# Sixteen of 22 gated blocks of a hybrid decoder layer transposed by DMA in uint16 halves

## The chip, the cores and the metric

The kernel runs on one core of one Trainium2 chip. The metric is the device time of one execution in microseconds (us), here the median of three runs. The matmul engine is called TensorE or PE, its weight load PEld, VectorE DVE, ScalarE ACT, GpSimd POOL; SP issues most DMAs, and SPq is its queue of instructions.

## The reference

One decoder layer on 256 tokens of width 2048, all in float32: a SwiGLU feed-forward, a mixer (windowed attention beside RWKV-7), cross-attention into a memory, a second SwiGLU feed-forward, a final norm. The change lies in the two feed-forwards:

```python
def swiglu(h, w_gate, w_up, w_down):
    return (jax.nn.silu(h @ w_gate) * (h @ w_up)) @ w_down
...
    x = x + 0.5 * swiglu(rms_norm(x, ffn1_norm[l]), ffn1_w_gate[l], ffn1_w_up[l], ffn1_w_down[l])
```

`w_gate` and `w_up` are 2048 x 5632 and `w_down` is 5632 x 2048.

## The kernel before

**Numbers in two parts.** Every float32 operand `v` of a matmul is split into `hi` (ACT's copy with type float32r, L370 for weights) and `lo = v - hi` (DVE, L371), and every product is three matmuls: hi by hi, lo by hi, hi by lo (L447 to L449).

**Blocks.** A feed-forward goes through its 5632 hidden columns in 11 blocks of 512, in three groups (4, 4 and 3). `gate_and_up` (L580) makes one block `hb`: 256 tokens by 512 columns, that is two tiles of 128 tokens (t = 0, 1). The tokens lie on the partitions. `down` (L608) multiplies a whole group by `w_down` and needs the hidden columns on the partitions, so each block is transposed in between, and then split into `hhi` and `hlo` by `split` (L642). The first block of a feed-forward comes from two plain products (L762 to L774).

**Eight steps of a block.** `product_pair` (L507) walks K = 2048 in eight steps, q = 0 to 7, of two 128-row slices of both weights. In the steps q of `SEVEN` it computes seven products in place of eight, from sums of weights that DVE makes (`raw`, L399 to L402), which are split as `thi` and `tlo` (L378, L379). In the first feed-forward these are q = 0, 2, 4; in the second q = 0, 2, 3, 4, where the sums of q = 3 were made earlier and are loaded from memory. Right after q = 4, `first` and `middle` (L585 to L593) take the seven-product banks off PSUM, and `out` (L595) closes the block after q = 7.

**Order of the work.** The program is recorded in one pass. Generators in groups (`Interleave`, L56) are stepped by `tick`, which the product calls some 29 times in a block; `idle(n)` lets n ticks pass. The tile framework then sets each engine's order from that record, and each engine executes in its order: an instruction that waits holds up all behind it on that engine. ACT and DVE prepare the parts of a weight one to two steps ahead of PE, in buffers (three for `hi` and `lo`, one for each of the `thi` and `tlo`) that PE has to release. SP loads 1 MB pieces of the weights into four buffers (`raw2`, tag of L311) as DVE releases them: one piece of the gate and one of the up weight feed two steps q.

**The transposes.** `transposed` (L750) calls `feat` (L632) twice, each with four PE transposes of 128 x 128 against `ident` into one PSUM bank, and `split` takes the banks. A block's generator is spawned in `middle` of the following block (L592), so its eight transposes stand on PE behind step q = 4 of that block. The last block of a group is transposed when `down` begins (L777). `sums_of` (L577) hands out `u` tiles, tag "u", two buffers; `hb` has two buffers.

Of the kernel before, what the change touches and what calls it, by code (L numbers as in the profile page):

```python
# [6 lines left out]

F32 = mybir.dt.float32
F32R = mybir.dt.float32r
AF = mybir.ActivationFunctionType  # L10
ALU = mybir.AluOpType
AX = mybir.AxisListType
# [3 lines left out]
P = 128  # L16
# [120 lines left out]
def decoder_layer(ctx: ExitStack, tc: tile.TileContext, a: dict, out: bass.AP):  # L137
    nc = tc.nc
    act, dve, pool, pe = nc.scalar, nc.vector, nc.gpsimd, nc.tensor
# [7 lines left out]
    bg = Interleave()  # L147
# [5 lines left out]
    bg.group("norm", 1)  # L153
    bg.group("mem", 1)
    bg.group("stage", 4)

    def f32(x):
        return x.bitcast(F32)
# [14 lines left out]
    def idle(n):  # L173
        for _ in range(n):
            yield
# [23 lines left out]
    def mixer_constants(sp):  # L199
# [70 lines left out]
    for entry in weight_plan(a):  # L270
# [4 lines left out]
        w, k0, nk, c0, n = entry  # L275
# [5 lines left out]
        for k in range(k0, k0 + nk, 2 * KU):  # L281
            u = len(units)
            units += [(v, k + i, c, 512) for v, c in zip(w, c0) for i in (0, KU)]
            for i in range(2):
                q = (k - k0) // KU + i
# [291 lines left out]
    def sums_of(sp):  # L577
        return (sp.tile([P, 512], F32, tag="u", name="u", bufs=2) for _ in range(2))

    def gate_and_up(sp, x: Act, c, r, w):  # L580

        hb = sp.tile([P, 2, 512], F32, tag="hb", name="hb", bufs=2)
        u2, u3 = sums_of(sp)

        def first(b):  # L585
            act.copy(hb[:, 0], b["p1"][:])

        def middle(b):
            dve.tensor_tensor(u2[:], b["p6"][:], hb[:, 0], ALU.add)
            dve.tensor_tensor(u3[:], b["p7"][:], u2[:], ALU.add)  # L590
            dve.tensor_tensor(u2[:], b["p5"][:], u2[:], ALU.add)
            while c["next"]:  # L592
                bg.spawn("feat", c["next"].pop())  # L593

        def out(b, to):  # L595
            t = int(to in ("p4", "p5"))
            if to in ("p2", "p4"):
                dve.tensor_tensor(hb[:, t], b[to][:], u3[:] if t else hb[:, 0], ALU.add)
                act.activation(hb[:, t], hb[:, t], AF.Silu, scale=r[t])
            else:  # L600
                v = u3 if t else u2
                dve.tensor_tensor(v[:], b[to][:], v[:], ALU.add)
                dve.scalar_tensor_tensor(hb[:, t], v[:], r[t], hb[:, t], ALU.mult, ALU.mult)

        product_pair(x, c, w, first, middle, out)
        return hb

    def down(h: Act, c, w, xs):  # L608
# [6 lines left out]
        def first(b):  # L615
            act.activation(x00, b["p1"][:], AF.Copy, scale=0.5)

# [24 lines left out]
    def split(x: Act, c, n, src):  # L642

        act.copy(x.at(0, c, n), src)
        dve.tensor_tensor(x.at(1, c, n), src, f32(x.at(0, c, n)), ALU.subtract)
        x.done |= set(range(c, c + n))
# [81 lines left out]
    def feed_forward(sp, x, norm: Norm, wg, wu, wd, done, begin_last=lambda: None, last=False):  # L728
        if last:
            for tag, shape, dt, bufs in (  # L730
                ("hhi", [P, 16, T], F32R, 1), ("hlo", [P, 16, T], F32R, 1),
                ("hb", [P, 2, 512], F32, 2), ("thia", [P, KU, 512], F32R, 1),
                ("tloa", [P, KU, 512], F32R, 1), ("thib", [P, KU, 512], F32R, 1),
                ("tlob", [P, KU, 512], F32R, 1),
            ):
                sp.tile(shape, dt, tag=tag, name=tag, bufs=bufs)
        begun = at["item"]
        c = combinations(
            sp, norm.x, SEVEN_2 if last else SEVEN, "c",
            lambda: at["item"] > begun + (4 if last else 7) and not (last and norm.r is None),  # L740
        )
        c["next"] = []
        for gi, (j0, nj) in enumerate(GROUPS):
            h = Act(
                [sp.tile([P, 16, T], F32R, tag="hhi", name="hhi")],
                [sp.tile([P, 16, T], F32R, tag="hlo", name="hlo")], 16,
            )
            ch = combinations(sp, h, SEVEN_DOWN[nj < 4], "d", early=False, n=12)

            def transposed(hb, c):  # L750
                banks = [feat(hb, [2 * q * P, (2 * q + 1) * P]) for q in range(2)]
                for q, b in enumerate(banks):
                    split(h, c + 2 * q, 2, b)
                    yield

            for j in range(j0, j0 + nj):
                if j > 0:
                    hb = gate_and_up(sp, norm.x, c, norm.r, wg)

                    c["next"].append(transposed(hb, 4 * (j - j0)))  # L760
                    continue
                pg = product(norm.x, wg)  # L762
                hb = sp.tile([P, 2, 512], F32, tag="hb", name="hb", bufs=2)
                if last:
                    for t in range(2):
                        act.activation(hb[:, t, :], pg[t][:], AF.Silu, scale=norm.r[t])
                pu = product(norm.x, wu, bank=acc if last else mm)
                bg.until(lambda: norm.r is not None)
                for t in range(2):
                    if not last:  # L770
                        act.activation(hb[:, t, :], pg[t][:], AF.Silu, scale=norm.r[t])
                    dve.scalar_tensor_tensor(
                        hb[:, t, :], pu[t][:], norm.r[t], hb[:, t, :], ALU.mult, ALU.mult
                    )  # L774
                c["next"].append(transposed(hb, 0))
            end = gi == len(GROUPS) - 1
            bg.spawn("feat", c["next"].pop())  # L777
            if end:
                begin_last()

            def col(t, n):
                return x[:, t, n * 512 : (n + 1) * 512]

            for n in (0, 2):
                if last and end and n:

                    whole = [(t, slice(0, 512)) for t in range(2)]
                    parts_ = [(t, slice(c, c + 256)) for t in range(2) for c in (0, 256)]
                    pieces = {2: whole, 3: parts_}
                    for m in (n, n + 1):  # L790
                        pd = product(h, wd, skew=m == 3)
                        for t, cs in pieces[m]:
                            dve.scalar_tensor_tensor(
                                col(t, m)[:, cs], pd[t][:, cs], 0.5, col(t, m)[:, cs],
                                ALU.mult, ALU.add,
                            )
                            done(m, t, cs)
                    continue
                down(h, ch, wd, [[col(t, n + i) for i in range(2)] for t in range(2)])
                if end:  # L800
                    done(n)
                    done(n + 1)
# [17 lines left out]
    with tc.tile_pool(name="f1", bufs=1, reuse_waits="tile") as sp:  # L820
# [8 lines left out]
        turned = f32(sp.tile([P, KD, T], F32R, tag="hlo", name="hlo")[:])  # L829
# [991 lines left out]
```

## Time and profile before

| | |
|---|---|
| median of 3 runs (lowest, highest) | 2215.75 us (2214.65, 2217.29) |
| the profiled execution | 2216.82 us |
| its span in the trace | 2215.1 us |
| busy: PE, PEld, DVE, ACT | 99%, 82%, 81%, 58% |
| PE transposes of `hb` | 176 (22 blocks of 8) |
| granted TensorE clock | 0.999 of full speed |

Busy time is the share of the span; matmuls are pipelined, so that the profile gives each some 390 ns though they start some 227 ns apart. The first feed-forward takes the first 660 us or so of the span, the second begins near 1520 us and ends with it.

### The profile page before, as it was taken

To read this page: it belongs to the slowest core of one execution; us is meant where nothing else is said; L and a number is where in the kernel's file an instruction comes from. 1 tells how busy PE (TensorE), PEld (TensorE's weight loads), DVE (VectorE), ACT (ScalarE), POOL (GpSimd) and SP (SyncE) were. 2 spreads that over 40 slices of the span, in tenths; PEclk is the share of its full clock that TensorE was granted. 3 is DMA by queue.
4 is the path that set the end of the run, shared out by engine and by line. 5 is a ranking of instruction groups with operands and counts; after the bars stand their busy time and mean duration, and the time that the engine had idled before them with its cause. 6 is when DMAs were issued, how large, how long until landed. Compare 5 with 4: busy or idle time off the path is not lost.

```text
span 2215.1 us, 28167 instructions
## 1 busy us (share of the span) xinstructions
PE 2200.8 (99%) x10520; PEld 1816.7 (82%) x10520; DVE 1802.6 (81%) x2316; ACT 1275.5 (58%) x1677; POOL 106.9 (5%) x184
## 2 busy tenths in 40 slices
PE   9999999999999999999999999999999999999998
PEld 7888888888888878888888888888888888888886
DVE  7998888998989476877667666558999899998996
ACT  7555555555556477644544546556565565655654
POOL 0000000000000001000321030001000000000000
PEclk9999999999999999999999999999999999999999
DMA  8555555565556545677778687558665666666573
GB/s 306 194 206 192 206 195 203 195 204 193 197 192 211 174 132 164 212 225 215 224 220 290 206 272 269 185 165 275 221 221 189 207 233 208 217 205 210 200 244 136
DMA packets 198280, 466.02 MB, mean 210 GB/s; under 512 B 15520, under 2 KB 17920, under 8 KB 187136
## 3 DMA queue, kind: packets, MB, share of 16 engines
q1 hardware_dynamic: 188976, 438.08, 59.2%
q0 software_dynamic: 7648, 23.52, 3.5%
q10 hardware_dynamic: 1520, 2.63, 0.3%
q8 instruction: 82, 1.34, 0.3%
q14 instruction: 54, 0.44, 0.1%
HBM read 440.49 MB, written 23.59 MB: 210 GB/s over the span
## 4 chain that ended last, share of the span: by engine, by line
PE 93%; DVE 3%; DMA 2%; ACT 1%; issue 1%; SPq 0%; POOLq 0%; POOL 0%; DVEq 0%; ACTq 0%
PE acc L447 19%; PE acc L448 19%; PE acc L449 19%; PE mm L447 8%; PE mm L448 8%; PE mm L449 8%; PE tr L639 2%; PE tr L448 2%; PE tr L447 2%; PE tr L449 2%; DMA raw<-in_ffn_w_up_dram 1%; DVE lo L371 1%; PE mm L1441 1%; DVE tlo L379 1%; PE tr L1371 0%
## 5 line engine op out<-in xcount | busy, mean ns | idle before, releaser
L370 ACT CAST hi<-raw 128x1024 fp32r<-128x1024 f32 (+1 forms) x768 | 754.6, 993 | 671.8 <-PE acc L449 483.1
L371 DVE TENSOR_TENSOR lo<-raw,hi 128x1024 fp32r<-128x1024 f32 (+1 forms) x768 | 879.4, 1149 | 314.9 <-ACT hi L370 312.4
L447 PE MATMUL acc<-hi,xhi 128*128 128x512 f32 (+1 forms) x1134 | 445.4, 394 | 1.9 <-ACT hi L672 1.1
L448 PE MATMUL acc<-lo,xhi 128*128 128x512 f32 (+1 forms) x1134 | 440.0, 388 | 1.6 <-DVE lo L371 1.5
L449 PE MATMUL acc<-hi,xlo 128*128 128x512 f32 (+1 forms) x1134 | 439.5, 388 | 0.0
L447 PEld LDWEIGHTS acc<-hi,xhi 128*128 128x128 f32 x1134 | 212.9, 188 | 47.4 <-issue 3.2
L448 PEld LDWEIGHTS acc<-lo,xhi 128*128 128x128 f32 x1134 | 213.0, 188 | 44.4 <-DVE lo L371 3.1
L449 PEld LDWEIGHTS acc<-hi,xlo 128*128 128x128 f32 x1134 | 212.9, 188 | 43.4 <-issue 0.4
L378 ACT CAST thi<-raw 128x1024 fp32r<-128x1024 f32 x192 | 199.9, 1051 | 64.8 <-DVE raw L401 44.4
L379 DVE TENSOR_TENSOR tlo<-raw,thi 128x1024 fp32r<-128x1024 f32 x192 | 232.3, 1218 | 0.9 <-ACT thi L378 0.3
L447 PE MATMUL mm<-hi,xhi 128*128 128x512 f32 x402 | 156.6, 389 | 0.0
L448 PE MATMUL mm<-lo,xhi 128*128 128x512 f32 x402 | 156.5, 389 | 0.0
L449 PE MATMUL mm<-hi,xlo 128*128 128x512 f32 x402 | 156.4, 389 | 0.0
L448 PE MATMUL acc<-lo,hhi 128*128 128x512 f32 x372 | 145.3, 391 | 0.0
L449 PE MATMUL acc<-hi,hlo 128*128 128x512 f32 x372 | 145.3, 391 | 0.0
L447 PE MATMUL acc<-hi,hhi 128*128 128x512 f32 x372 | 145.0, 390 | 0.0
L447 PEld LDWEIGHTS mm<-hi,xhi 128*128 128x128 f32 x402 | 75.5, 188 | 16.2 <-ACT hi L370 0.5
L448 PEld LDWEIGHTS mm<-lo,xhi 128*128 128x128 f32 x402 | 75.5, 188 | 15.8
L449 PEld LDWEIGHTS mm<-hi,xlo 128*128 128x128 f32 x402 | 75.5, 188 | 15.6
L448 PEld LDWEIGHTS acc<-lo,hhi 128*128 128x128 f32 x372 | 69.8, 188 | 14.4
L447 PEld LDWEIGHTS acc<-hi,hhi 128*128 128x128 f32 x372 | 69.9, 188 | 14.3
L449 PEld LDWEIGHTS acc<-hi,hlo 128*128 128x128 f32 x372 | 69.9, 188 | 14.0
(441 smaller groups left out, 3527.4 us busy)
## 6 DMA issues: line engine op xcount, KB each, us to landing
raw<-in_ffn_w_down_dram SPq DMA_DIRECT2D x88, 1024.0 KB, 5.2
raw<-in_ffn_w_gate_dram SPq DMA_DIRECT2D x84, 1024.0 KB, 5.1
raw<-in_ffn_w_up_dram SPq DMA_DIRECT2D x78, 1024.0 KB, 5.8
raw<-in_w_in_dram SPq DMA_DIRECT2D x136, 512.0 KB, 3.8
raw<-in_w_out_dram SPq DMA_DIRECT2D x32, 512.0 KB, 4.8
raw<-sums SPq DMA_DIRECT2D x20, 512.0 KB, 6.3
raw<-in_w_proj_attn_dram SPq DMA_DIRECT2D x16, 512.0 KB, 4.3
raw<-in_w_proj_rwkv_dram SPq DMA_DIRECT2D x16, 512.0 KB, 6.0
```

The lines of the kernel that those rows point to most:

```text
L370: at["hi"] = act.copy(hi[:, s], raw[:, s])
L371: at["lo"] = dve.tensor_tensor(lo[:, s], raw[:, s], f32(hi[:, s]), ALU.subtract)
L378: act.copy(hi[:], v[:])
L379: dve.tensor_tensor(lo[:], v[:], f32(hi[:]), ALU.subtract)
L447: pe.matmul(o, xh, hi, start=first, stop=False, **how)
L448: pe.matmul(o, xh, lo, start=False, stop=False, **how)
L449: pe.matmul(o, xl, hi, start=False, stop=last, **how)
L639: pe.transpose(b[:, o : o + P], tok[:, t, col : col + P], ident[:])
L1441: pe.matmul(vb[to, (o + k) * P : (o + k + 1) * P][:, r], lhs(k, e), v[:, k, r], start=v is u and k + e == 0, stop=True, **ek,)
```

## The change

Sixteen blocks (the first three of the groups of four, the first two of the groups of three, in both feed-forwards) take `turned` in place of `transposed`; the last of each group stays with PE. `turned` reads the float32 block as pairs of uint16 (`e` = 0, 1). ACT copies each half of all words into a `uh` tile of its own (L761: two copies of 128 x 1024). SP then issues four DMA transposes (L767: for each half and each token tile, 128 x 512 uint16 into four blocks of 128 x 128) into `ht`, which has a buffer of `hb`. Seven ticks later ACT writes the halves back beside each other into float32 tiles `u` (L772: four copies of 128 x 512 uint16), and `split` works from these. The generator is spawned when the next block begins, not in its step q = 4, in a group of its own, and `hb`, `u2`, `u3` are taken only in `first`, when it has run out.

```diff
@@ -153,6 +154,7 @@
     bg.group("stage", 4)
+    bg.group("turn", 1)
...
     def gate_and_up(sp, x: Act, c, r, w):
 
-        hb = sp.tile([P, 2, 512], F32, tag="hb", name="hb", bufs=2)
-        u2, u3 = sums_of(sp)
+        hb, u2, u3 = None, None, None
+        while c["next"]:
+            bg.spawn("turn", c["next"].pop())
 
         def first(b):
+            nonlocal hb, u2, u3
+            bg.until(lambda: not bg.groups["turn"][1])
+            hb = sp.tile([P, 2, 512], F32, tag="hb", name="hb", bufs=2)
+            u2, u3 = sums_of(sp)
             act.copy(hb[:, 0], b["p1"][:])
 
         def middle(b):
...
-            while c["next"]:
-                bg.spawn("feat", c["next"].pop())
...
+            def turned(hb, c):
+
+                both = hb[:].rearrange("p t n -> p (t n)")
+                src = both.bitcast(U16).rearrange("p (t n e) -> p e t n", t=2, e=2)
+                us = [sp.tile([P, 2, 512], U16, tag="u", name="uh", bufs=2) for _ in range(2)]
+                for e, u in enumerate(us):
+                    act.copy(u[:], src[:, e])
+                    yield
+                dst = sp.tile([P, 2, 2, 4, P], U16, tag="hb", name="ht", bufs=2)
+                yield
+                for e, u in enumerate(us):
+                    for t in range(2):
+                        nc.sync.dma_start(dst[:, e, t], u[:, t], transpose=True)
+                yield from idle(7)
+                for q, u in enumerate(sums_of(sp)):
+                    v = u[:].bitcast(U16).rearrange("p (c t k e) -> p e t c k", c=2, t=2, e=2)
+                    for e in range(2):
+                        act.copy(v[:, e], dst[:, e, :, 2 * q : 2 * q + 2, :])
+                    split(h, c + 2 * q, 2, u[:].rearrange("p (c t) -> p c t", c=2))
+                    yield
...
-                    c["next"].append(transposed(hb, 4 * (j - j0)))
+                    turn = transposed if j == j0 + nj - 1 else turned
+                    c["next"].append(turn(hb, 4 * (j - j0)))
...
-                c["next"].append(transposed(hb, 0))
+                c["next"].append(turned(hb, 0))
```

What it does to the order is shown at one block of the first feed-forward, the third of its first group (j = 2), while it computes: the block before it is the one that is transposed. On SP before, the loads for that block and the next, gate and up by turns:

```order
L324 DMA raw2_817<-in_ffn1_w_gate_dram 128x2048 [waits DMAHW6_49,DVE_49]
L324 DMA raw2_876<-in_ffn1_w_up_dram 128x2048 [waits DMAHW7_49,DVE_49]
L324 DMA raw2_914<-in_ffn1_w_gate_dram 128x2048 [waits DMAHW0_49,DVE_49]
L324 DMA raw2_962<-in_ffn1_w_up_dram 128x2048 [waits DMAHW1_49,DVE_49]
L324 DMA raw2_993<-in_ffn1_w_gate_dram 128x2048 [waits DMAHW2_49,DVE_49]
```

On SP now, the same loads (`raw2_914` is now `raw2_921`, `raw2_962` is `raw2_973`):

```order
L326 DMA raw2_878<-in_ffn1_w_up_dram 128x2048 [waits DMAHW7_49,DMAHW3_49,DVE_49]
L326 DMA raw2_921<-in_ffn1_w_gate_dram 128x2048 [waits DMAHW0_49,DMAHW4_49,DVE_49,Activation_49]
L767 DMA_TRANSPOSE ht_916<-uh_896 128x4x128 [waits Activation_49]
L767 DMA_TRANSPOSE ht_916<-uh_896 128x4x128
L767 DMA_TRANSPOSE ht_916<-uh_897 128x4x128 [waits Activation_49]
L767 DMA_TRANSPOSE ht_916<-uh_897 128x4x128
L326 DMA raw2_973<-in_ffn1_w_up_dram 128x2048 [waits DMAHW5_49,DVE_49]
```

The four transposes stand between the gate piece and the up piece of the steps q = 4, 5.

On ACT now, at the same place, from the taking apart to the putting together (before, only the weight casts `hi` and `thi` stood here):

```order
L761 COPY uh_896<-hb_735 128x1024 [waits DVE_49]
L761 COPY uh_897<-hb_735 128x1024
L372 CAST hi_933<-raw2_822 128x1024 [waits DMAHW6_49,PE_49,Activation_49]
L380 CAST thi_929<-raw_923 128x1024 [waits DVE_49]
L372 CAST hi_937<-raw2_878 128x512 [waits DMAHW7_49,PE_49,Activation_49]
L380 CAST thi_941<-raw_924 128x1024 [waits DVE_49]
L772 COPY u_1034<-ht_916 128x2x2x128 [waits DMAHW2_49,DMAHW1_49,Activation_49]
L372 CAST hi_975<-raw2_822 128x1024 [waits PE_49]
L772 COPY u_1034<-ht_916 128x2x2x128 [waits DMAHW4_49,DMAHW3_49]
L772 COPY u_1051<-ht_916 128x2x2x128 [waits Activation_49]
L649 CAST hhi_146<-u_1034 128x512 [waits Activation_49]
```

The second `uh` copy and four weight casts lie between the first `uh` copy and the first `u` copy, which waits for transposes; the fourth `u` copy, two weight casts, the second `hhi` and then the `thi` of q = 4 follow.

On DVE before, the work for q = 3, 4 behind the `lo` of the step q = 3:

```order
L371 TENSOR_TENSOR lo_965<-raw2_817,hi_964 128x1024 [waits Activation_49]
L399 TENSOR_TENSOR raw_996<-raw2_962,raw2_914 128x512 [waits DMAHW5_49,DMAHW4_49]
L400 TENSOR_TENSOR raw_995<-raw2_962 128x512
L401 TENSOR_TENSOR raw_995<-raw2_962,raw_996 128x512 [waits DVE_49]
L371 TENSOR_TENSOR lo_969<-raw2_876,hi_968 128x1024 [waits Activation_49]
L402 TENSOR_TENSOR raw_996<-raw2_914,raw_995 128x512 [waits DVE_49]
L379 TENSOR_TENSOR tlo_1002<-raw_995,thi_1001 128x1024 [waits Activation_49]
```

On DVE now:

```order
L373 TENSOR_TENSOR lo_976<-raw2_822,hi_975 128x1024 [waits Activation_49]
L650 TENSOR_TENSOR hlo_147<-u_1034,hhi_146 128x512 [waits Activation_49]
L401 TENSOR_TENSOR raw_1007<-raw2_973,raw2_921 128x512 [waits DMAHW5_49,DMAHW0_49]
L373 TENSOR_TENSOR lo_980<-raw2_878,hi_979 128x1024 [waits Activation_49]
L402 TENSOR_TENSOR raw_1006<-raw2_973 128x512
L403 TENSOR_TENSOR raw_1006<-raw2_973,raw_1007 128x512 [waits DVE_49]
L373 TENSOR_TENSOR lo_1017<-raw2_921,hi_1016 128x1024 [waits Activation_49]
L404 TENSOR_TENSOR raw_1007<-raw2_921,raw_1006 128x512 [waits DVE_49]
L381 TENSOR_TENSOR tlo_1013<-raw_1006,thi_1012 128x1024 [waits Activation_49]
```

The first `hlo` of the turned block now stands ahead of the sums for q = 4, and a `lo` ahead of their `tlo`; before, both `hlo` came behind q = 4.

More of the change, by code (lines that the diff above doesn't have):

```diff
@@ L9 @@
 F32R = mybir.dt.float32r
+U16 = mybir.dt.uint16
 AF = mybir.ActivationFunctionType
```

## The prediction

> **What bounds the kernel now.** I read the page's totals and its chain that ended last, then the waits of TensorE alone.
>
> ```profile
> span 2215.1 us, 28167 instructions
> PE 2200.8 (99%) x10520; PEld 1816.7 (82%) x10520; DVE 1802.6 (81%) x2316; ACT 1275.5 (58%) x1677; POOL 106.9 (5%) x184
> PE 93%; DVE 3%; DMA 2%; ACT 1%; issue 1%; SPq 0%; POOLq 0%; POOL 0%; DVEq 0%; ACTq 0%
> PE acc L448 <- DVE lo L371: 1.8, 4, 0.7
> ```
>
> TensorE is the bound: 99% busy, 93% of the chain, and its longest kind of wait adds up to 1.8 us in the whole span. So an instruction that leaves TensorE shortens the kernel, as long as what feeds it keeps up. Whether it does is read from the feed-forward, by the windows of two blocks of the first one and of a stretch of the second.
>
> ```profile
> 80.50:122.90 42.40, 42.40 (x194) 35.21 (x192) 38.27 (x46) 24.17 (x27) 0.00 (x0) 1.00 0.56 201
> 122.90:165.40 42.50, 42.50 (x193) 35.14 (x192) 39.77 (x52) 25.61 (x31) 0.00 (x0) 1.00 0.56 195
> 1840.00:1880.00 40.00, 40.00 (x181) 32.67 (x180) 39.16 (x49) 24.57 (x28) 0.00 (x0) 1.00 0.68 230
> 1880.00:1920.00 40.00, 40.00 (x181) 32.76 (x180) 39.26 (x49) 26.15 (x32) 0.00 (x0) 1.00 0.68 230
> ```
>
> After the stretch and its length come PE, PEld, DVE and ACT busy. DVE has 4.1 and 2.7 us of a block free in the first feed-forward, and 0.8 us of 40 in this part of the second: it nearly binds beside TensorE. ACT has some 16 us of a block free. So the gain is small room on TensorE, and every wait put in front of DVE is paid from little.
>
> **The gain.** The eight transposes of a block on the chain, and what TensorE does next:
>
> ```profile
> 122.45 0.87 PE tr L639 x8
> 123.32 0.23 PE acc L447
> ```
>
> 0.87 us a block, x 16 blocks = **13.9 us** off TensorE. That is the most the change can bring, 0.63%. It bounds the time from below at 2216.8 - 13.9 = 2202.9 us, counted against the profiled execution; that lies 1.1 us above the median of the runs shown, so a median could be 2201.9.
>
> **ACT's added work.** The rows nearest to the new copies, and those of DVE that move with them:
>
> ```profile
> L370 ACT CAST hi<-raw 128x1024 fp32r<-128x1024 f32 x662 | 688.8, 1052 | 601.9 <-PE acc L449 447.2 <-PE mm L449 122.4 <-issue 8.7
> L644 ACT CAST yrhi<-yq 128x512 fp32r<-128x512 f32 x4 | 2.5, 620 | 0.7 <-DVE yq L1554 0.7
> L645 DVE TENSOR_TENSOR hlo<-tr,hhi 128x512 fp32r<-128x512 f32 x44 | 28.7, 686 | 3.8 <-ACT hhi L644 3.3
> L479 DVE TENSOR_TENSOR raw<-hhi,hlo x16: 682/684/687, 127.0 to 2147.4; 128x512 f32<-128x512 f32 x16
> L488 DVE TENSOR_TENSOR raw<-raw x23: 281/284/294, 31.7 to 2150.4; 128x128 f32<-128x128 f32 x23
> ```
>
> A block adds two copies of 1024 columns (1.05 each) and four of 512 (0.62): 4.6 us, and each `hhi` reads SBUF (620 ns) in place of PSUM. No row here has a uint16 at every second place; I take the float32 times. Half of them, or twice, would be 2.3 or 9.2 us: either fits into ACT's free 16, so the amount costs nothing. What counts is where they stand. DVE's `hlo` (0.69) and the sums for `down` (L479, 0.68, and three of 0.28) move and keep their size.
>
> **SP and the transposes.** In the block shown with the order, the pieces for q = 4, 5 and the gate piece for q = 6, 7 were issued at
>
> ```profile
> 99.17 0.33 SPq L324 DMA_DIRECT2D raw<-in_ffn_w_gate_dram  x1
> 101.07 0.33 SPq L324 DMA_DIRECT2D raw<-in_ffn_w_up_dram  x1
> 108.55 0.33 SPq L324 DMA_DIRECT2D raw<-in_ffn_w_gate_dram  x1
> raw<-in_ffn_w_gate_dram SPq DMA_DIRECT2D x84, 1024.0 KB, 5.1
> raw<-in_ffn_w_up_dram SPq DMA_DIRECT2D x78, 1024.0 KB, 5.8
> dl<-ld SPq DMA_DIRECT2D x4, 128.0 KB, 4.4
> L1262 SPq DMA_DIRECT2D dl<-ld x4: 339/618/1690, 943.5 to 946.3; - x4
> DMA to landing us min/median/max: 4.2/4.4/5.0
> ```
>
> The trace has no DMA transpose. The nearest row is `dl`: 128 KB like one transpose, in 1024 pieces of 128 bytes. It held SP for 0.34 to 1.69 us (median 0.62) and landed 4.2 to 5.0 us after issue. A transpose reads 512 rows of 256 bytes and scatters them finer, so below the median is unlikely; I take the middle between `dl`'s median and its longest, **1.15 us of SP each, landing 4.4 us after issue**, and keep 0.34/4.2 and 1.69/5.0 as ends.
>
> The Trainium skill ("Advanced Engine Details and Errata", X-Bar Transpose (TRN2)) says that transpose DMAs are as fast as regular ones; by that the four would cost what the lower end gives. No run so far shows it.
>
> **One block of the first feed-forward, step by step.** ACT and DVE there, before:
>
> ```profile
> 98.73 2.00 ACT L370 CAST hi<-raw 128x1024 fp32r<-128x1024 f32 x2 [1.67 <-PE acc L449]
> 108.44 0.68 DVE L399 TENSOR_TENSOR raw<-raw,raw 128x512 f32<-128x512 f32 x1
> 111.98 1.22 DVE L379 TENSOR_TENSOR tlo<-raw,thi 128x1024 fp32r<-128x1024 f32 x1
> 117.50 1.23 DVE L371 TENSOR_TENSOR lo<-raw,hi 128x1024 fp32r<-128x1024 f32 x1 [1.42 <-ACT hi L370]
> 116.39 0.39 PE L448 MATMUL tr<-tlo,chi 128*128 128x512 f32 x1
> 121.15 0.39 PE L448 MATMUL acc<-lo,xhi 128*128 128x512 f32 x1
> ```
>
> - The `uh` copies take the place behind the first cast of the pair at 98.73: 99.7 to 100.7 and to 101.7.
> - SP issues the four transposes from 100.7 on, 4 x 1.15: free at 105.3, the last one issued at 104.2 and landed at **108.6**.
> - The up piece, until now issued at 101.07, goes out at 105.3, 4.2 later, and lands 5.1 to 5.8 later, 110.4 to 111.1. The piece behind it on SP was not issued before 108.55 anyway.
> - On ACT two `u` copies (one waited, one more) and `hhi` follow the last landing, 3 x 0.6: 110.4. DVE's first `hlo` ends at 111.1. It stands ahead of the sums for q = 4, and these need the up piece as well. Both release them at about 111.1, where before they began at 108.44: **2.7 us late**.
> - From 108.44 on DVE ran without a gap past the `tlo` at 111.98 (done at 113.2), which TensorE first needed at 116.39: 3.2 us in hand. Now 113.2 + 2.7, and 1.1 for the `lo` that stands ahead of it: 117.0. **TensorE waits 0.6 us.**
> - Behind it come the remaining `lo` and `tlo` (1.8), and newly L479, the second `hlo` and the three small sums (2.1) ahead of the `lo` that stood at 117.50: it ends near 122.0 where 121.15 + 0.6 is needed, some 0.2 more.
>
> Together **0.8 us lost** against 0.87 gained: eight such blocks give -0.5 us. Not each is the same (the first of a group has no sums for `down`), but DVE keeps less than 4 us of a block to catch up, so a late block hands lateness on.
>
> **The second feed-forward.** There q = 3 and q = 4 are both seven-product steps, and the `u` copies fall between them on ACT:
>
> ```profile
> 1861.61 1.06 ACT L378 CAST thi<-raw 128x1024 fp32r<-128x1024 f32 x1 [0.30 <-PE mm L449]
> 1864.33 1.74 ACT L370 CAST hi<-raw 128x512 fp32r<-128x512 f32 x2 [1.66 <-DVE tlo L379]
> 1865.97 2.00 ACT L378 CAST thi<-raw 128x1024 fp32r<-128x1024 f32 x2
> 1867.76 2.35 DVE L379 TENSOR_TENSOR tlo<-raw,thi 128x1024 fp32r<-128x1024 f32 x2
> 1867.08 0.72 PE L447 MATMUL tr<-thi,chi 128*128 128x512 f32 x2
> 1869.04 0.50 PE L448 MATMUL tr<-tlo,chi 128*128 128x512 f32 x1
> ```
>
> TensorE used the `thi` and the `tlo` within 0.1 us of their making, so nothing is in hand at this place. Between the casts at 1861.61 and 1865.97 ACT was idle for 1.66 us and busy otherwise; four copies and two `hhi` (3.4 us when pipelined) come in: the `thi` is some 1.7 us later, of which the new order of TensorE's matmuls hides a part and DVE, that did other things meanwhile, half. I take 0.9 between the ends 0 and 1.7. The landing itself is late by less than ACT's place, which is eight instructions behind the `uh` copies. Eight blocks: 8 x (0.9 - 0.87) = +0.2 us.
>
> **Sum:** -13.9 + 8 x 0.8 + 8 x 0.9 = -0.3 us: 2216.5 against the profiled execution, about 2215.5 against the median. I forecast **2216 us, no change that counts**. (About 0.2%, 4.4 us, is what a measurement of this kernel can tell from none.) With the losses of a block anywhere from a half to one and a half of what I took, this case covers 2208 to 2223.
>
> **Rivals.**
>
> *The transposes are cheap, the gain stays.* With 0.34 us of SP and 4.2 of landing the last transpose (behind the second `uh` copy) is issued at 102.0 and landed at 106.3; the up piece goes out at 102.4 and lands at 108.2. DVE is at most 0.4 us late, inside its 3.2. The first feed-forward keeps 8 x 0.87 = 7.0; the second keeps between nothing and 7.0. 2203 to 2210. For it: these are ordinary queue entries of 128 KB. Against it: the fine pieces.
>
> *Slower: SP is held by the transposes, and the weights behind them come late.* With 1.69 us each and 5.0 of landing, the last is issued at 105.8 and landed at 110.8, `hlo` ends at 113.3, and the up piece goes out at 107.5 and lands at 113.3. That is 2.2 us beyond the 111.1 above, and as the 3.2 in hand are already spent, all of it reaches TensorE, in the second feed-forward too, where gate, sums and up piece are loaded in a bunch. 16 x 2.2 = 35: about 2251. It decides from the point at which four transposes hold SP longer than some 4.6 us or land later than 108.6. Speaking for it: DVE already waits for this very kind of load.
>
> ```profile
> L399 DVE TENSOR_TENSOR raw<-raw,raw 128x512 f32<-128x512 f32 x86 | 59.0, 686 | 17.3 <-DMA raw<-in_ffn_w_up_dram 14.4 <-DMA raw<-in_ffn_w_down_dram 2.8
> ```
>
> *Slower by far: the transposes run one after another.* Each landing 4.4 us behind the one before, the last is there at 100.7 + 17.6 = 118.3, 9.7 late: 16 x 9.7 = 155, 2371 us. The order shows no wait from one to the next, which speaks against it. The Trainium skill ("Vector Engine: DVE Perf Modes", The three transpose paths) gives 1309 ns for one 128 x 128 block by DMA and 390 on TensorE; 16 blocks in a row would be an estimated 21 us by that page, near this rival. This trace has eight float32 ones on TensorE in 0.87 us.
>
> That the change doesn't do what it says is excluded: only the last blocks' transposes, 48 of 176, stand on TensorE now, and 64 DMA transposes on SP.
>
> **Chances.** Forecast case 0.42 (faster 0.10, same 0.20, slower 0.12); cheap transposes 0.27, all faster; SP held 0.26 and one after another 0.05, slower. Faster 0.37, same 0.20, slower 0.43. The range goes from the full gain, 2203, to a little past the second rival, 2255; above it lie the serial case and the late end of the held one, about 0.15, and below 0.02.
>
> **What would show it.** In the changed profile: SPq's time of one DMA_TRANSPOSE (1.15) and its landing (4.4); the wait of ACT's `u` copies for `ht`, at most 2 us a block; DVE's L401 waiting for the up piece some 2 us more than before; TensorE's waits for `tlo` and `lo` up from 2 us in all to about 14. It would be wrong if ACT's uint16 copies took a multiple of the float32 ones, if the transposes slowed the weight loads by their traffic, or if the halves' scattered writes disturbed DVE.

## The result and the profile after

| | before | changed |
|---|---|---|
| median (lowest, highest), four runs each | 2216.1 us (2214.7, 2217.3) | 2248.1 us (2246.2, 2251.8) |
| ratio to before, 95% interval | | **1.0147** [1.0129, 1.0164] |
| span of the profiled execution | 2215.1 us | 2250.1 us |

The changed kernel is 32 us, 1.5%, slower. The forecast, no change that counts, was wrong, and its own case ended at 2223 us. The stated range, 2203 to 2255, holds the measured time only because it was drawn to take in the second rival; that rival's mechanism, with its 2251 us, is what came.

The page's totals and the chain that ended last, of the changed kernel:

```profile
span 2250.1 us, 28118 instructions
PE 2205.8 (98%) x10392; PEld 1803.5 (80%) x10392; DVE 1800.1 (80%) x2316; ACT 1341.4 (60%) x1773; POOL 107.0 (5%) x184
PE 76%; DVE 12%; DMA 6%; ACT 2%; issue 2%; SPq 1%; POOLq 0%; POOL 0%; ACTq 0%; DVEq 0%
```

TensorE has 128 instructions less, as planned, and yet its share of the chain went from 93% to 76%. DVE and DMA stand in it now: TensorE waits for parts of weights that are late. Its own waits say for which (us in total, times, longest):

```profile
PE acc L450 <- DVE lo L373: 8.3, 10, 1.1
PE tr L449 <- ACT thi L380: 6.6, 10, 1.4
PE tr L450 <- DVE tlo L381: 5.8, 8, 1.3
PE acc L449 <- ACT hi L372: 4.7, 5, 1.6
```

These four kinds have 25.4 us; all of TensorE's waits of a matmul for DVE or ACT add up to some 33 us, where before there were 4 to 5. What the change added, by the groups of ACT (busy us and mean ns of one, then the idle time ahead of them), and by the transposes' own line on SP (nanoseconds least, median, most):

```profile
L761 ACT COPY uh<-hb 128x1024 uint16<-128x1024 uint16 x32 | 32.5, 1044 | 7.0 <-DVE hb L608 5.4 <-DVE hb L799 1.6
L772 ACT COPY u<-ht 128x512 uint16<-128x512 uint16 x64 | 47.3, 770 | 19.0 <-DMA ht<-uh 18.9
```

```profile
L767 SPq DMA_TRANSPOSE ht<-uh x64: 1188/1281/2969, 59.9 to 2143.4; - x64
DMA to landing us min/median/max: 2.4/5.0/8.3
```

A transpose holds SP for 1.28 us (median); all 64 together for 91.7 us (the sum of their rows in SP's timeline), 5.7 us a block. How that reaches TensorE is seen in the block behind the one of the order excerpts (j = 3, the last of its group), by the timelines of SP, DVE, ACT and PE (start, duration, and in brackets the idle time before with what ended it). On SP at the same place before:

```profile
142.71 0.33 SPq L324 DMA_DIRECT2D raw<-in_ffn_w_gate_dram  x1
143.81 0.33 SPq L324 DMA_DIRECT2D raw<-in_ffn_w_up_dram  x1
```

Now, on SP, DVE, ACT and PE:

```profile
148.68 0.33 SPq L326 DMA_DIRECT2D raw<-in_ffn_w_gate_dram  x1
150.02 5.59 SPq L767 DMA_TRANSPOSE ht<-uh  x4
155.72 0.52 SPq L326 DMA_DIRECT2D raw<-in_ffn_w_up_dram  x1
```

```profile
159.38 1.23 DVE L373 TENSOR_TENSOR lo<-raw,hi 128x1024 fp32r<-128x1024 f32 x1 [2.09 <-ACT hi L372]
162.30 0.69 DVE L401 TENSOR_TENSOR raw<-raw,raw 128x512 f32<-128x512 f32 x1 [1.69 <-DMA raw<-in_ffn_w_up_dram]
```

```profile
156.14 2.30 ACT L772 COPY u<-ht 128x512 uint16<-128x512 uint16 x3 [0.83 <-DMA ht<-uh]
164.23 1.04 ACT L380 CAST thi<-raw 128x1024 fp32r<-128x1024 f32 x1 [2.09 <-DVE raw L403]
```

```profile
165.32 0.50 PE L449 MATMUL tr<-thi,chi 128*128 128x512 f32 x1 [0.92 <-ACT thi L380]
167.12 0.66 PE L450 MATMUL tr<-tlo,chi 128*128 128x512 f32 x1 [1.29 <-DVE tlo L381]
```

The up piece of q = 4, 5 leaves 5.7 us behind the transposes' start, and 7.0 us behind the gate piece, where it was 1.1 before. DVE stands for it until 162.30, though it had stood for 2.09 us already for a cast that ACT did behind the `u` copies. From L401 the lateness goes through L403, `thi` and `tlo` to TensorE, which waits 0.92 and 1.29 us. The windows of the block of the order excerpts (j = 2) and of this one show the price (stretch, length, then PE, PEld, DVE, ACT and POOL busy, granted clock, DMA share, GB/s):

```profile
82.00:124.50 42.50, 41.84 (x184) 34.27 (x184) 37.14 (x45) 28.28 (x34) 0.00 (x0) 1.00 0.65 211
124.50:170.80 46.30, 43.96 (x184) 35.23 (x183) 40.66 (x54) 29.44 (x36) 0.00 (x0) 0.96 0.62 193
```

Before, these two blocks took 42.4 and 42.5 us. So j = 2 lost what it was to gain and hardly more, and j = 3 stands 3.8 us above its old time. Two waits end in j = 3, then, and the totals do not say which of them sets the time: SP held, so that the weights are late (**theory A**), or ACT standing at `u` until the halves have landed, with the casts of the next piece behind it (**theory C**). **Theory B** lays it to ACT's 5 us of added copies and the order that they force.

### The profile page after: what moved, and what is told of

It is laid out like the page before. It is cut to its first block, busy times and chain, and to the rows that moved or that the text cites. A ratio compares the mean times of both kernels' runs of the same rounds, so it can differ in the third digit from the quotient of the medians.

```text
span 2250.1 us, 28118 instructions
## 1 busy us (share of the span) xinstructions
PE 2205.8 (98%) x10392; PEld 1803.5 (80%) x10392; DVE 1800.1 (80%) x2316; ACT 1341.4 (60%) x1773; POOL 107.0 (5%) x184
## 4 chain that ended last, share of the span: by engine, by line
PE 76%; DVE 12%; DMA 6%; ACT 2%; issue 2%; SPq 1%; POOLq 0%; POOL 0%; ACTq 0%; DVEq 0%
PE acc L449 17%; PE acc L450 17%; PE acc L451 17%; PE mm L449 5%; PE mm L451 5%; PE mm L450 5%; DVE lo L373 4%; DMA raw<-in_ffn_w_up_dram 3%; DVE tlo L381 2%; DMA ht<-uh 1%; PE tr L644 1%; PE tr L450 1%; PE tr L451 1%; PE tr L449 1%; PE mm L1468 1%
## 5 line engine op out<-in xcount | busy, mean ns | idle before, releaser
L450 PEld LDWEIGHTS mm<-lo,xhi 128*128 128x128 f32 x402 | 75.7, 188 | 15.6
L449 PEld LDWEIGHTS acc<-hi,hhi 128*128 128x128 f32 x372 | 69.9, 188 | 14.2
```

The lines of the kernel that those rows point to most:

```text
L449: pe.matmul(o, xh, hi, start=first, stop=False, **how)
L450: pe.matmul(o, xh, lo, start=False, stop=False, **how)
```

## The experiments

Three measures go through all of them, each from the timelines. The *mark* is `first`'s copy into `hb` (L593; L586 before). From a mark of the first feed-forward to the issue of the third up piece behind it (q = 4, 5) it is 25.0 us before and 29.3 us changed, **4.3 us late** on the mean of seven blocks; to the third L401, which needs that piece, 32.3 and 35.7, **3.4 us late**. The *first stretch* goes from DVE's first `hb<-mm` (57.44 us into the changed kernel) to the last mark of the first feed-forward (642.05) and holds eight transposed blocks; the *second stretch*, from the first mark to the last of the second feed-forward, holds seven.

### The transposition left out

`turned` does no copy and no transfer; `split` takes the halves of `hb` one tick later than they would have been put together (eleven ticks are let pass, where the changed kernel lets ten).

```diff
-                us = ...; act.copy(u[:], src[:, e]) ...; dma_start(..., transpose=True)
+                yield from idle(11)
+                for q in range(2):
+                    split(h, c + 2 * q, 2, hb[:, q]...)
+                    yield
```

> The 16 blocks are neither copied, sent nor transposed: L649/L650 take the halves straight from hb at the same tick at which the changed kernel would put them together (the transposition is left out, so the values are in the wrong places). Every theory expects the forecast's gain alone, 16 x 0.87 = 13.9 us under before: 2202, within 2198 to 2206. If it stays at 2230 or more, what costs is neither the copies nor the transfers but the new group of background steps and the later free hb and u buffers, and all theories below fall.

Measured: 2205.5 us, ratio 0.9955 [0.994, 0.9969]. That is 10.6 us under before, not 13.9. The first stretch gave what was counted: 562.9 us against 569.6, 6.8 for eight blocks. In the second seven blocks gave 2.2 us of 6.1 (543.6 against 545.8). There `split` comes later than TensorE's own transposes allowed it, its `hlo` and the sums for `down` stand among the `lo`, and TensorE waits 5.0 us in all for `lo`, where the last block of a group is computed and at `down`; before, it did not wait for `lo` there at all.

### ACT's copies without transfers

L761 writes into the buffer that L772 reads.

```diff
-                    act.copy(u[:], src[:, e])
+                    act.copy(dst[:, e].rearrange("p t c k -> p t (c k)"), src[:, e])
...
-                        nc.sync.dma_start(dst[:, e, t], u[:, t], transpose=True)
```

> The copies L761 and L772 stay, but L761 writes its halves straight into the buffer that L772 reads, so that no transfer stands between them (the transposition is left out). Theory A (the four transposes hold SP for 5.1 to 5.7 us, the up piece behind them is late, and L401 and all behind it with it): the loss is gone, 2202 to 2208. Theory B (ACT's 5.2 us of added copies and the order that they force on ACT and DVE): the loss stays, 2238 to 2250. Theory C (the copies L772 wait for the landing and hold ACT): gone as under A, 2202 to 2208.

Measured: 2209.9 us, ratio 0.9972 [0.9962, 0.9983]. ACT's copies with their order cost 4.4 us over the run without them, in which `split` came that one tick later. With the copies kept and the transfers gone the kernel is 6.2 us under before: theory B does not carry the loss. The transfers cost 2248.1 - 2209.9 = **38.2 us**: of the two stretches, 584.6 against 564.0 us in the first, 561.1 against 545.5 in the second, 36.2 together.

### The transposes behind the up piece

```diff
                 dst = sp.tile([P, 2, 2, 4, P], U16, tag="hb", name="ht", bufs=2)
-                yield
+                yield from idle(5)
...
-                yield from idle(7)
+                yield from idle(max(7-4,1))
```

> The transposes are issued three ticks later, so that on SP they stand behind the up piece (q = 4, 5) instead of ahead of it; all else is as in the changed kernel, and the copies L772 stand at the same tick. Theory A: L401 no longer waits for its load, most of the 46 us of added waits goes, 2206 to 2218. Theory B: no change, 2245 to 2251. Theory C: the landing is 0.5 to 1 us later, ACT waits longer at L772: 2250 to 2265.

(The transposes come four ticks later, and the copies L772 keep their tick, since `idle(max(7-4,1))` lets three pass; but in ACT's order two or more casts of the next piece now pass ahead of them. In seven of the eight blocks of the first feed-forward the first of the four transposes still goes ahead of the up piece and three behind it.) Measured: 2222.6 us, ratio 1.0031 [1.0021, 1.0041]: 25.5 of the 32 us are back, though it ends 4.6 us above what theory A expected. SP's timeline in the block at 102 us, where all four go behind, and what ACT and DVE waited for in all:

```profile
101.79 0.33 SPq L326 DMA_DIRECT2D raw<-in_ffn_w_up_dram  x1
102.17 6.28 SPq L767 DMA_TRANSPOSE ht<-uh  x4
```

```profile
ACT u L772 <- DMA ht<-uh: 28.6, 18, 4.7
DVE raw L401 <- DMA raw<-in_ffn_w_up_dram: 21.2, 20, 2.2
```

The changed kernel's line for L401:

```profile
DVE raw L401 <- DMA raw<-in_ffn_w_up_dram: 20.0, 22, 2.7
```

SP is held longer than before, ACT stands 28.6 us at L772 in place of 18.9, and L401's own wait is no shorter: by these totals it should be slower. But the up piece goes out 25.1 us after the mark, and L401 starts at 32.8. L401's wait was no measure: an instruction that comes late for another reason waits less for its load.

### Plain copies in place of the transposes

```diff
-    nc.sync.dma_start(dst[:, e, t], u[:, t], transpose=True)
+    nc.sync.dma_start(dst[:, e, t], u[:, t].rearrange("p (c k) -> p c k", c=4))
```

> The four transposes of a block become four plain copies of the same 128 KB from uh to ht on the same queue at the same place (the transposition is left out). A load of 1 MB holds SP for 0.33 us, so the four should hold it for some 1.3 to 2 us in place of 5.1 to 5.7. Theory A: the up piece is at most 2 us late and most of the loss goes: 2206 to 2216. Theory B: 2240 to 2250. Theory C: by the landing of a plain copy (some 2 to 3 us in place of 5.0): 2205 to 2220. A theory D, that the transposes' small packets slow the loads beside them, expects 2205 to 2216 as well, and is told from A by the run in which the transposes stand behind the up piece, where D leaves 2245 and more.

Measured: 2228.2 us, ratio 1.0054 [1.0039, 1.0069], outside what every theory had expected: above A and C, below B.

```profile
L767 SPq DMA_DIRECT2D ht<-uh x64: 470/596/1786, 58.2 to 2117.2; - x64
DMA to landing us min/median/max: 2.0/5.5/8.2
```

A plain copy of 128 KB inside SBUF holds SP for 0.60 us, half a transpose, and lands no earlier (5.5 us against 5.0). With the four ahead of it the up piece is out at 26.4. The first stretch is only 3.5 us over the run without transfers: 1.4 us of lateness against the kernel before find their slack there. The second is 11.9 over: as the forecast read it, nothing is in hand in that one. The Trainium skill ("Advanced Engine Details and Errata", X-Bar Transpose (TRN2)) says that transpose DMAs are as fast as regular ones: of the landing the two runs agree with it, of SP's time they do not.

### SP held, with nobody waiting for the data

The run without transfers; in the first feed-forward, four transposes of `ht` go from the same place on SP into buffers that are never read.

```diff
+                if not last:
...
+                    for i, to in enumerate([junk[:, 0], junk[:, 1], junk[:, 2], four]):
+                        nc.sync.dma_start(to, dst[:, i // 2, i % 2], transpose=True)
```

> As the run whose copies L761 write straight into L772's buffer (2209.9), and beside it, in the 8 blocks of the first feed-forward, the four transposes are issued at the changed kernel's place, from that buffer into one that nobody reads: SP is held, and nothing waits for the landing (the outputs hold no transposition; the second feed-forward has no transposes at all). There the changed kernel is 21.8 us behind that run at the last copy of the first feed-forward (642.05 against 620.24). Theory A (SP held, up piece late): most of it comes back, that copy at 634 to 642, in all 2224 to 2232. Theory C (ACT's queue stands at L772 until the halves land, and the casts of the next piece behind it): nothing comes back, 620 to 624, in all 2209 to 2214.

Measured: 2225.6 us, ratio 1.0047 [1.003, 1.0064]. The last mark of the first feed-forward, in the changed kernel, in the run without transfers and in this one:

```profile
642.05 0.59 ACT L593 COPY hb<-mm 128x512 f32<-128x512 f32 x1 [1.30 <-PE mm L451]
```

```profile
620.24 0.59 ACT L593 COPY hb<-mm 128x512 f32<-128x512 f32 x1 [0.93 <-PE mm L451]
```

```profile
633.58 0.59 ACT L593 COPY hb<-mm 128x512 f32<-128x512 f32 x1 [1.30 <-PE mm L451]
```

13.3 of the 21.8 us come back by the held SP alone. (The three differ by up to 2 us at DVE's first `hb<-mm` already, ahead of all transposes; without that it is 14.2 of 20.7.) The up piece goes out at 28.9, L401 starts at 35.2. The rest is not told apart by this run, since its order on ACT is another one.

### The plain copies from GpSimd's queue

```diff
-    nc.sync.dma_start(dst[:, e, t], u[:, t]...)   # the run with plain copies
+    pool.dma_start(dst[:, e, t], u[:, t]...)
```

> The run with four plain copies in place of the transposes (2228.2, SP held 2.46 us a block, ACT waits 8.8 us in all for their landing), with the copies issued by GpSimd, which is idle in the feed-forwards (the transposition is left out). Theory A: the loads go out on time, and the time falls to that of the run without transfers, 2208 to 2214. Theory C: the landing is what ACT waits for, so it stays at 2222 to 2230, or rises if GpSimd's copies land later. Theory B, what is left to ACT's copies: not under 2209.

Measured: 2280.1 us, ratio 1.029 [1.0275, 1.0305]. The loads go out on time (L401's wait is 11.6 us in all, 14.4 before), but the copies land late, and ACT pays:

```profile
DMA to landing us min/median/max: 4.2/6.8/9.1
```

```profile
ACT u L772 <- DMA ht<-uh: 66.9, 24, 6.1
PE tr L449 <- ACT thi L380: 16.6, 11, 4.0
```

So C exists and can cost more than A: with SP free, a landing 1.8 us later (6.8 against 5.0) put 66.9 us of waiting on ACT ahead of `thi`. (Part of the 70 us over the run without transfers is the clock: seven times in the feed-forwards, from the first transposed block on, the granted clock was halved, as the last section shows it for the changed kernel.) That it also acts in the changed kernel, beside A, I took from this and from the rest that the run before had left; the run with the copies behind the casts tested it, and it fell.

### One transpose for each half

```diff
-                    for t in range(2):
-                        nc.sync.dma_start(dst[:, e, t], u[:, t], transpose=True)
+                    nc.sync.dma_start(dst[:, e]... "p (t c) k", u[:]... "p (t n)", transpose=True)
```

> One transpose for each half (128x1024) in place of two (128x512): the same bytes in 32 instructions in place of 64. If an instruction has a price of its own, SP is held 2.6 us a block in place of 5.1 to 5.7 and the last half lands some 2.5 us earlier; theories A and C both expect some half of the 38 us that the transfers cost then, 2225 to 2236. If the price goes by the bytes, SP is held 5 us and more and the time stays, 2244 to 2252. Theory B: no change, 2245 to 2251.

Measured: 2236.1 us, ratio 1.0091 [1.0076, 1.0106]. The price goes partly by the instruction: two hold SP for some 2.5 us in five of the eight blocks of the first feed-forward, but for 4.4 to 4.7 in the other three, and 65.2 us in all. The Trainium skill ("DMA: Bandwidth & Descriptors", Rules for kernel authors) advises to join small transfers into large ones; 32 in place of 64 gave 12 us here.

Here the up piece goes out at 27.4 on the mean, 25.4 to 27.4 in the blocks where SP is held for 2.5 us and 28.4 to 30.0 in the others; the first stretch is 11.0 us over the run without transfers, the second 12.5.

### The copies behind the casts

```diff
+                    with tc.issue_after(at["hi"].ins):
                         for e in range(2):
                             act.copy(v[:, e], dst[:, e, :, 2 * q : 2 * q + 2, :])
```

> As the changed kernel, with one thing moved: the copies L772 may be issued only after the newest cast L372 of the program at that place, so that on ACT they stand behind the casts of the next piece in place of ahead of them; SP is untouched, the four transposes still stand ahead of the up piece. Theory A alone (SP held): nothing changes, 2245 to 2251. Theory C alone (ACT held at L772): back to the run without transfers, 2208 to 2214. A and C side by side, as the last runs have it (in the first feed-forward 13 us of 21.8 by the held SP, the rest by the landing): the landing's part goes, 8 to 9 us there and as much in the second feed-forward, 2228 to 2236.

Measured: 2245.6 us, ratio 1.0128 [1.0115, 1.0142]. ACT never waits for `ht` now, and 2.5 us are gained, not 12 to 20: **C as a cost beside A falls.** (The run also puts the turned halves later, and what that costs by itself is not measured apart.) The wait is DVE's now, for the same late piece:

```profile
DVE raw L401 <- DMA raw<-in_ffn_w_up_dram: 48.2, 32, 3.6
PE tr L450 <- DVE tlo L381: 7.6, 13, 1.2
```

20.0 us of that wait became 48.2. The up piece goes out at 28.1, and the first stretch is still 18.7 us over the run without transfers. In the changed kernel ACT's wait for the landing had run beside the wait for the load; with one taken away the other comes forward. Theory A alone had given 2245 to 2251.

### Both moves, and where the copies stand

The first two have `idle(5)` ahead of the transposes and `idle(7)` ahead of the copies, so that these come four ticks later than in the changed kernel; the third has `idle(5)` twice, two ticks later; the last mixes the two.

> Both moves together: three of the four transposes behind the up piece on SP, and the copies L772 behind the casts of the next piece on ACT. A and C side by side: both parts go, and what is left is ACT's own time, 2209 to 2217, within 0.3 per cent of the kernel before. Theory A alone: as the run with the first move only, 2220 to 2225. If it stays above 2225, a third cost is open.

Measured: 2227.1 us, ratio 1.0047 [1.0035, 1.006]; slower than the first move alone. Five of the seven blocks of the first feed-forward that have marks on both sides lose 0.6 us or less against the run without transfers. But the copies now stand behind `first`'s copy L593, and at the ends of the groups, in the last block of a group of four and at `down`, the turned halves come late to the sums for `down`, and TensorE waits some 1.6 us each time there. Its waits of this kind in the whole span:

```profile
PE acc L450 <- DVE lo L373: 14.6, 13, 1.6
```

> A version meant to beat both: only the 8 blocks of the first feed-forward are transposed by DMA, with one transpose for each half, behind the up piece where the order lets it, and the copies behind the casts; the second feed-forward keeps TensorE's transposes as in the kernel before. There the copies without transfers are 5.3 us ahead of the kernel before at the last copy of the first feed-forward (620.24 against 625.51), which is the floor: 2211 to 2215 where A and C are the whole cost; 2216 to 2222 if the transposes cost something besides.

Measured: 2226.2 us, ratio 1.0038 [1.0024, 1.0051], outside both ranges. The same placing, the same loss: the last mark of the first feed-forward stands at 632.18, and at 633.11 in the run before. The second stretch takes 545.9 us, as before the change (545.8).

> The run with both moves (2227.1) with its copies L772 two ticks earlier: on ACT they stand behind the casts of the next piece still, but ahead of the copy L593 that opens the next product, in place of behind it. In that run the blocks that follow another gate-and-up product lose next to nothing (0 to 0.5 us each), and some 12 us go at the ends of the groups of the first feed-forward, where the halves that come late feed the sums of the down product. If that placing is the third cost, it goes here and the held SP and the landing stay away: 2211 to 2218. If the rest is due to the transfers themselves (their traffic, SP held 6 to 8 us even behind the up piece), it stays at 2224 to 2230.

Measured: **2215.9 us, ratio 1.0000 [0.9991, 1.0009]**. (The expectation says that L593 opens the next product; it is `first`'s copy behind q = 4.) SP in the block at 144 us, and the waits that are left:

```profile
144.24 0.33 SPq L326 DMA_DIRECT2D raw<-in_ffn_w_up_dram  x1
144.63 6.39 SPq L767 DMA_TRANSPOSE ht<-uh  x4
```

```profile
ACT u L773 <- DMA ht<-uh: 0.4, 1, 0.4
DVE raw L401 <- DMA raw<-in_ffn_w_up_dram: 23.7, 25, 2.2
PE acc L450 <- DVE lo L373: 5.0, 9, 0.9
```

SP is still held, for 5 us a block and longer, and L401 still waits 23.7 us in all; but the up piece goes out at 24.2 and L401 starts at 32.0, much as before the change (25.0 and 32.3), and TensorE's waits for `thi` and `tlo` are down to 1.3 us in all.

> As the run with both moves, with the earlier place of the copies only in the last block of a group that DMA transposes in the first feed-forward, where that run lost; everywhere else its own late place, at which the second feed-forward took no longer than the run without transfers (545.5 us between the first copies of its first and last block in both). If the place at the groups' ends is the third cost: 2211 to 2217, by the floor of 2209.9 and some 1 to 5 us of rest. If not: 2223 to 2230.

Measured: 2219.4 us, ratio 1.0015 [1.0006, 1.0024], between the two ranges. The second stretch kept its 545.7 us. In the first, the stretches in which the third blocks of both groups of four are transposed lost by the change of place within a group (46.4 and 47.7 us from mark to mark, 42.2 and 42.5 in the run before); why was not tested. The second stretch took 545.5 with the later place, 550.0 with the earlier; but behind its last mark the later place takes 95.4 us to the end and the earlier 91.6, so that the earlier place in the first feed-forward and the later in the second would be an estimated 2215, the time before. That version was not run, and no version measured here, with the transposes by DMA, beats the kernel before.

The two moves, each with and without the other:

| | transposes ahead of the up piece | behind it |
|---|---|---|
| copies free | 2248.1 | 2222.6 |
| copies behind the casts | 2245.6 | 2215.9 |

(The copies of the last come two ticks later in the program than those of the run to its left; on ACT they stand at the same place but for one cast.) Moving the transposes is worth 25.5 and 29.8 us, moving the copies 2.5 and 6.7. Most of the loss is the place in SP's queue; the copies' place is worth little until that is mended.

The measures of the first feed-forward side by side, for the runs that do not lose by a late place of the copies:

| | up piece out after the mark | L401 | first stretch over the run without transfers |
|---|---|---|---|
| without transfers | 24.7 | 31.6 | 0 |
| both moves, 2215.9 | 24.2 | 32.0 | 6.0 |
| behind the up piece | 25.1 | 32.8 | 5.7 |
| plain copies | 26.4 | 34.4 | 3.5 |
| one for each half | 27.4 | 34.9 | 11.0 |
| copies behind the casts | 28.1 | 33.8 | 18.7 |
| never read | 28.9 | 35.2 | 14.2 |
| changed kernel | 29.3 | 35.7 | 20.7 |

The loss follows the issue of the piece: 3 to 6 us up to 26.4, 11 to 21 from 27.4 on. L401 follows it less well: with the copies behind the casts it starts earlier than with plain copies (33.8 against 34.4), and yet 18.7 us are lost there and 3.5 here. What else carries the loss in that run is not shown.

The same pieces show whether the load itself is slowed. From issue to landing the up piece takes, on the mean of the seven blocks, 6.1 us before, 6.2 without transfers and 6.1 in the changed kernel: there it is late by its issue alone. With the transposes behind it, it takes 7.5 us, in the run with the first move and in the one of 2215.9: some 1.3 us of the earlier issue is lost again on the way.

## Why the prediction was wrong, point by point

- **The case that was forecast.** It was to end between 2208 and 2223 us and had a chance of 0.42; the rival that came had 0.26. Over all cases the forecast gave a slower kernel 0.43, a faster one 0.37 and no change 0.20: its headline, no change that counts, was the least likely of the three by its own chances.
- **The gain, 13.9 us.** Measured 10.6. Nearly exact in the first feed-forward (6.8 us for eight blocks, 0.85 each, forecast 0.87); in the second most of it went with the later place of `split`, which the forecast had not priced apart.
- **ACT's copies, "the amount costs nothing".** They cost 4.4 us. L761 takes 1.04 us as forecast, L772 0.77 in place of 0.62, 5.2 us a block in place of 4.6.
- **SP, 1.15 us a transpose and landing 4.4.** 1.28 at the median, 1.43 at the mean (91.7 / 64), landing 5.0; 5.7 us a block, past the 4.6 from which the rival was to decide. "The up piece goes out 4.2 later": 4.3.
- **L401 2.7 us late against 3.2 in hand, 0.8 us lost a block.** This is the step that failed, and not in the block that the forecast walked through: there (j = 2) L401 was 2.0 us late, TensorE waited 0.7 us for `tlo`, and the block took 42.6 us from mark to mark where it had taken 42.4. 3.4 us on the mean is near the 2.7, too; but the first stretch lost 20.7 us by the transfers, 2.6 a block. What failed is the factor eight: the forecast took one lateness for all blocks. Against the kernel before, L401 was 2.0 to 3.0 us late in four of the seven, and these took 0.5 to 1.8 us longer from mark to mark than without transfers, about what 0.8 had said; in the other three it was 4.5 to 5.0 late, and they took 2.6, 3.9 and 4.7 longer. The first block, which is not among the seven, took 4.6. Two of the three are the last that a group transposes, where "a late block hands lateness on", as the forecast said and did not put into the sum.
- **The second feed-forward, 0.9 us lost a block.** Its reading, nothing in hand, held: even the plain copies cost 1.7 a block there. The transposes cost 15.6 us over seven blocks, 2.2 each, beyond the 1.7 that the forecast had taken for the late end. It had counted ACT's place there and not the late weights; the first move, on SP alone, takes 7.8 of the 15.6 us back, both moves 11.1, and the copies behind the casts alone none.
- **The sum.** -10.6 by TensorE, +4.4 by ACT, +38.2 by the transfers: +32.0, where the forecast had -13.9 + 13.6.
- **The rivals.** "SP is held by the transposes, and the weights behind them come late" was the mechanism, and its 2.2 us a block, net, is near the measured 32.0 / 16 = 2.0. That the number came so near is in part luck: it took 1.69 us a transpose where 1.43 was measured (by the rows, with the gaps between them), let L401 start 4.9 us late in every block where the mean was 3.4, and left out ACT's 4.4 us and the 3.3 us that the gain fell short. The cheap transposes did not come. Nor did the serial ones: the last of four had landed 9.4 us after the first was issued, on the mean of the 16 blocks, not 17.6.
- **The signs.** TensorE's waits rose to some 33 us, not 14. ACT's wait for `ht` is 1.2 us a block, within the 2 forecast, and still told nothing, since it hid behind the other. "L401 waiting some 2 us more" a block would be 32 us; it waits 20.0 in all against 14.4, and the run that gives all the time back has 23.7.

What stays open is what the run with the copies behind the casts loses by, beside the late piece, and why the version with both moves stands 6 us above the run without transfers. The 1.3 us by which its up piece lands slower may be part of it; no run changed the traffic alone.

## What to carry to other kernels

When DMAs are put on a queue that also loads the weights, count the issuing engine's time as well as the landing, and place them behind the load that is due next; here that order alone decided 25 to 30 us of 32. To judge which of two waits binds, take one away and see whether the time falls or the other wait grows; totals of waits misled here, while the issue of the late load, counted from a mark in its block, parted the runs that lost little from those that lost much. And a slack read in one block is to be tried on the latest block of a chain, not on the mean.

## What the runs showed of the hardware

**SP pays for each transpose.** 1.28 us for one of 128x512 uint16, 0.60 for a plain copy of the same bytes within SBUF, 0.33 for a load of 1 MB of weights (the row at 148.68). The cost is not one of bytes.

**A uint16 copy at every second place is slower only by a quarter when it writes so.** L772, which writes the halves at every second place, takes 0.77 us for 512 columns, where a float32 row of that length took 0.62; L761, which reads them so, takes 1.04 for 1024, as a float32 cast of that length.

**A wait of TensorE can cost more than itself.** After the 0.92 and 1.29 us above, the changed kernel's TensorE starts matmuls 0.43 us apart, not 0.23, for some 3 us:

```profile
168.00 0.63 PE L449 MATMUL tr<-thi,chi 128*128 128x512 f32 x1
168.43 0.63 PE L450 MATMUL tr<-tlo,chi 128*128 128x512 f32 x1
...
170.13 0.63 PE L451 MATMUL mm<-hi,xlo 128*128 128x512 f32 x1
170.56 0.47 PE L449 MATMUL acc<-hi,xhi 128*128 128x512 f32 x1
```

Eight starts were 0.2 us late each, 1.6 us, with 0.96 as the granted clock of that window. The Trainium skill ("TensorE: Matmul & The Clock Gate", Part 1) gives 426.7 ns between the starts of 512 columns while the clock is gated to half, and these rows agree. It happened twice in the changed kernel's feed-forwards, some 3 us of its 32, and not in the version with both moves that equals the kernel before.
